# The adaLN matrices laid out transposed and summed along rows on VectorE; five weight strips opened at the start; weights stored strip by strip

## The chip, the cores and the metric

One core of a Trainium2 chip runs one launch of one kernel. The time is that of the device, in microseconds (us), from the first to the last instruction of the launch. The kernel before took 2402.32 us, the median of three runs (2398.26 to 2405.06). Layouts that numpy makes of the inputs before the launch are not in that time.

## The reference

One layer of a hybrid network, batch 1, 2048 tokens, width 1024, all float32. A vector `c` (1 x 1024) gives, through SiLU and two matrices, eight vectors of 1024: three for the mixing half, three for the feed-forward half, two for the last norm.

```
c_act = silu(c)
mod = c_act @ w_ada + b_ada                      # 1024 -> 6 x 1024
shift_m, scale_m, gate_m, shift_f, scale_f, gate_f = split(mod, 6)
h = rms_norm(x, g_norm_mix) * (1 + scale_m) + shift_m
p = h @ w_in                                     # 1024 -> 3592: 28 strips of 128 columns, and 8 columns a, beta
#   k, q, v: causal depthwise conv over 4 tokens, SiLU, gated delta rule in chunks; z gates it
#   gate_b, gate_c, h_conv: gated causal conv over 3 tokens, group norm
x = x + gate_m * (concat(ya, yb) @ w_out)
h = rms_norm(x, g_norm_ffn) * (1 + scale_f) + shift_f
gt, up = split(h @ w_gate_up, 2)                 # 1024 -> 2 x 2816
x = x + gate_f * ((silu(gt) * up) @ w_down)
shift_o, scale_o = split(c_act @ w_ada_final + b_ada_final, 2)
out = rms_norm(x, g_norm_final) * (1 + scale_o) + shift_o
```

## The kernel before

Tokens are worked in four blocks of 512. Every wide product is made of float32 operands split in two parts of the fp32r type, high and low (`whi`, `wlo` of a weight strip, `hTh`, `hTl` of the input), and three TensorE matmuls for each tile: high x high, high x low, low x high. A strip is 1024 x 128 weights; against one block of tokens it takes 8 x 3 matmuls of 128x512 into one PSUM bank (`pd`, four banks; `pm`, four more for everything else). A strip is loaded by SyncE's queue into one of four slots `wraw`, cast to `whi` by ScalarE (L389), and VectorE subtracts to get `wlo` (L391); `whi` and `wlo` have four slots each. PE's dense matmuls all stand on line L322, in a helper.

**The start.** The columns `Gm` and `Sm` (gain and shift of the first norm, feature along the partitions) need 2 x 1024 x 1024 numbers of `w_ada`. They come in three parts of 3, 3 and 2 feature blocks (`PARTS`). Of each part, eight pieces (k = 0 to 7) of 384 or 256 columns for the scale and eight for the shift are loaded. Their rows are the summed index, so VectorE multiplies each piece by a column of `silu(c)` and adds it to an accumulator (L802, L804); a matmul with ones then sums over the partitions (L483, `col_sums`). The very first part is done on TensorE instead, as 24 matmuls of one column (L796). `part_norm` then transposes the normed input (L568), ScalarE scales and shifts it in PSUM (L572) and casts it to `hTh` (L573), VectorE subtracts for `hTl` (L574). Four strips (the k heads) are "opened": after each part their matmuls for that part's feature blocks run; `proj_ab` does the 8 extra columns. After that each strip's PSUM bank goes through a convolution on VectorE (L1246, L1248 three times, L1250).

**The background.** The other six vectors are made by `mod_gen`: one piece of 128 rows x 1024 columns is loaded at each call of `fill`, between the weight strips and in the same `wraw` slots (later in the `y` slots), and added to an accumulator by VectorE (L467 first, then L469). At the end `to_col` sums over the partitions by ones (L483), or `to_row` adds the bias on one row (L505), splits the accumulator (L513) and spreads it by ones over all partitions (L516, L517, L532, L533).

**What sets the order.** Small chains of work are generators that run between the matmuls; a class `Clock` keeps a table of costs, decides by it when a generator may run, and pins the order of every engine's instructions from the k heads of the first block to the end of the mixing half. So an engine's order is fixed at build time, and an instruction that is late holds up what stands behind it. SyncE issues the loads in that order too; at most eight are under way, since each waits for the semaphore of an earlier one.

Of the kernel before, what the change touches and what calls it, by code (L numbers as in the profile page):

```python
# [40 lines left out]
HALF = 1024  # L41

# [168 lines left out]
def layer_kernel(ctx, tc, x, c, w_ada, b_ada, w_ada_final, b_ada_final, g_norm_mix, g_norm_ffn, g_norm_final,  # L211
                 w_in, conv_w_mix, conv_w_qkv, a_log, dt_bias, g_conv_out, g_dn_out, w_out, w_gate_up,
# [3 lines left out]
    w_ada, w_in, w_out, w_gate_up, w_down = w_ada[0], w_in[0], w_out[0], w_gate_up[0], w_down[0]  # L216
# [111 lines left out]
    crow = sp.tile([P, BLK], F32, name="ht", bufs=2)[:KD, :P]  # L328
    nc.scalar.dma_start(crow, c.rearrange("o (j p) -> (o j) p", p=P))
# [14 lines left out]
    nc.gpsimd.memset(g0.tile([P, 32], F32, name="pad"), 0.0)  # L344
# [3 lines left out]
    col = {}  # L348

    def columns(name, queue, rows):  # L350
        r0, n_all = 0, sum(cnt for _, _, cnt in rows)
        prow = sp.tile([P, BLK], F32, name="ht", bufs=2)[:n_all, :P]
        pc = g0.tile([P, n_all], F32, name=name)
        for n, ap, cnt in rows:
            queue.dma_start(prow[r0:r0 + cnt, :], ap)
            col[n] = pc[:, r0:r0 + cnt]
            r0 += cnt
        return prow, pc

    def turn(prow, pc):  # L360
        pt = misc_ps()
        n = pc.shape[1]
        nc.tensor.transpose(pt[:, :n], prow, ident[:n, :n])
        nc.scalar.copy(pc, pt[:, :n])

    cols_a = columns("pca", nc.scalar, [("b_ada", b_ada.rearrange("o (j p) -> (o j) p", p=P), 48),
                                        ("g_mix", g_norm_mix.rearrange("o (j p) -> (o j) p", p=P), 8),
                                        ("g_ffn", g_norm_ffn.rearrange("o (j p) -> (o j) p", p=P), 8)])
    for i, n in ((0, "b_sm"), (1, "b_cm"), (3, "b_sf"), (4, "b_cf")):
        col[n] = col["b_ada"][:, i * KD:(i + 1) * KD]  # L370

    pcs = misc_ps()
    nc.tensor.transpose(pcs[:, :KD], crow, ident[:KD, :KD])
    cs = g0.tile([P, KD], F32, name="cs")
    nc.scalar.activation(cs, epsc.to_broadcast([P, KD]), AF.Silu)
    nc.scalar.activation(cs, pcs[:, :KD], AF.Silu)
    turn(*cols_a)


    lo_engines = deque()  # L380
# [1587 lines left out]
```

## Time and profile before

| | |
|---|---|
| median of the runs shown | 2402.32 us (2398.26 to 2405.06) |
| the profiled execution's own time | 2403.85 us |
| its span in the profile | 2402.1 us |
| PE, PEld, DVE, ACT, POOL busy, share of the span | 97%, 81%, 74%, 44%, 24% |
| mean granted TensorE clock | 0.994 |
| read from and written to HBM | 265.74 MB, 75.51 MB |

PE is TensorE's matmul, PEld its weight load, DVE VectorE, ACT ScalarE, POOL GpSimd, SP SyncE. Times within the profile are us from the start of the span, where they are not marked ns. A row of a timeline gives start, duration, engine, line, operation, the tile written, the tiles read, shape and count, and in brackets the idle time before it and what ended that. A row of groups gives the count, then busy us and mean ns of one, then the idle time before. A row of windows gives the stretch and its length, then for PE, PEld, DVE, ACT and POOL the busy us and the instructions (x), then the granted clock, the busy share of the 16 DMA engines and the GB/s moved.

### The profile page before, as it was taken

Reading aid. Unit: us, or ns where it says so; the run is one execution under the profiler, and the core shown is the slowest. Engines: PE = TensorE matmul, PEld = TensorE weight load, DVE = VectorE, ACT = ScalarE, POOL = GpSimd, SP = SyncE. Lnnn points to the kernel's source line nnn. Section 1 sums busy time; section 2 is a strip of 40 time slices with the busy share of each in tenths; the row PEclk is TensorE's granted clock in tenths of the full one; section 3 lists DMA queues with packets and bytes.
Section 4 is the critical chain, followed back from the end, with each engine's and each line's share of the span. In section 5 each row is a group of like instructions: output and inputs, shape, how many; then the busy total and the mean of one; then the engine's idle time right before and its main releaser. Section 6 shows DMA issues by size and latency. Waiting matters only on the chain.

```text
span 2402.1 us, 31013 instructions
## 1 busy us (share of the span) xinstructions
PE 2341.1 (97%) x11317; PEld 1939.5 (81%) x11317; DVE 1788.3 (74%) x2673; ACT 1051.7 (44%) x1790; POOL 571.4 (24%) x643
## 2 busy tenths in 40 slices
PE   6999999999999999999999999999999999999998
PEld 5788888887888788887778888878888877887786
DVE  5988889775987678787556556875656569878888
ACT  3644664344544473366433334433333323322345
POOL 0340344033513161211000000000000036434447
PEclk9999999999999999999999999999999999999999
DMA  7443565535463445156664334753433374333433
GB/s 252 123 118 89 171 189 165 147 106 166 136 167 115 126 135 145 47 168 174 209 185 119 101 106 117 251 162 88 128 97 110 101 241 163 106 123 119 136 129 151
DMA packets 401136, 341.20 MB, mean 142 GB/s; under 512 B 39811, under 2 KB 343180, under 8 KB 400918
## 3 DMA queue, kind: packets, MB, share of 16 engines
q1 hardware_dynamic: 399430, 336.75, 45.9%
q0 software_dynamic: 1152, 2.10, 0.6%
q8 instruction: 89, 1.46, 0.2%
q14 instruction: 65, 0.53, 0.1%
q10 hardware_dynamic: 400, 0.36, 0.0%
HBM read 265.74 MB, written 75.51 MB: 142 GB/s over the span
## 4 chain that ended last, share of the span: by engine, by line
PE 66%; DVE 16%; DMA 7%; ACT 4%; issue 4%; POOL 2%; SPq 0%; ACTq 0%; DVEq 0%; POOLq 0%
PE pd L322 41%; PE pm L322 17%; DVE wlo L391 3%; DVE cv L1248 2%; DVE acc L1822 1%; DMA wraw<-in_w_in_dram 1%; ACT whi L389 1%; DMA y<-xT 1%; DVE wraw L469 1%; POOL wraw L1751 1%; DVE cv L1246 1%; PE pm L1082 1%; DMA A12d<-y 1%; DMA acc<-x 1%; PE pm L1090 1%
## 5 line engine op out<-in xcount | busy, mean ns | idle before, releaser
L389 ACT CAST whi<-wraw 128x1024 fp32r<-128x1024 f32 x286 | 299.7, 1050 | 404.5 <-PE pd L322 174.5
L391 DVE TENSOR_TENSOR wlo<-wraw,whi 128x1024 fp32r<-128x1024 f32 x286 | 361.9, 1266 | 98.4 <-ACT whi L389 94.2
L322 PE MATMUL pd<-hTh,whi 128*128 128x512 f32 x888 | 359.3, 406 | 0.6 <-ACT hTh L573 0.6
L322 PE MATMUL pd<-hTl,whi 128*128 128x512 f32 x888 | 346.9, 391 | 0.6 <-DVE hTl L574 0.6
L322 PE MATMUL pd<-hTh,wlo 128*128 128x512 f32 x888 | 347.2, 391 | 0.0
L322 PEld LDWEIGHTS pd<-hTh,wlo 128*128 128x128 f32 x888 | 166.8, 188 | 36.5 <-issue 0.3
L322 PEld LDWEIGHTS pd<-hTh,whi 128*128 128x128 f32 x888 | 167.3, 188 | 32.2 <-ACT hTh L573 1.0
L322 PEld LDWEIGHTS pd<-hTl,whi 128*128 128x128 f32 x888 | 167.6, 189 | 30.9 <-DVE hTl L574 1.1
L1616 POOL TENSOR_TENSOR wraw<-wraw 128x1024 f32<-128x1024 f32 x2 | 4.9, 2466 | 782.2 <-DMA wraw<-in_w_down_dram 773.8
L1564 DVE TENSOR_TENSOR sg<-sg,pd 128x512 f32<-128x512 f32 x44 | 30.2, 686 | 169.8 <-PE pd L322 169.8
L1822 DVE TENSOR_TENSOR acc<-acc,pd 128x512 f32<-128x512 f32 x192 | 127.4, 679 | 25.9 <-PE pd L322 24.3
L1702 ACT CAST xh<-ra 128x640 fp32r<-128x640 f32 (+1 forms) x85 | 60.4, 722 | 183.8 <-PE pm L322 134.6
L1248 DVE SCALAR_TENSOR_TENSOR cv<-pd,pcb,cv 128x511 f32<-128x511 f32 (+2 forms) x173 | 129.3, 748 | 5.2
L1711 POOL TENSOR_TENSOR xl<-ra,xh 128x640 fp32r<-128x640 f32 (+1 forms) x37 | 62.9, 1699 | 144.7 <-ACT xh L1702 144.7
L1822 DVE TENSOR_TENSOR acc<-acc,pm 128x512 f32<-128x512 f32 x120 | 81.7, 681 | 18.5 <-PE pm L322 18.1
L322 PE MATMUL pd<-whi,ym 128*128 128x512 f32 x256 | 84.8, 396 | 0.0
L1751 POOL TENSOR_TENSOR wraw<-wraw 128x512 f32<-128x512 f32 x40 | 70.0, 1772 | 46.9 <-DMA wraw<-in_w_down_dram 46.9
L322 PE MATMUL pd<-A22h,whi 128*128 128x512 f32 x176 | 70.4, 400 | 5.6 <-DVE sg L1564 5.6
L322 PE MATMUL pm<-S4h,whi 128*128 128x512 f32 x176 | 68.6, 390 | 1.3 <-ACT sg L1558 1.3
L322 PE MATMUL pd<-A22l,whi 128*128 128x512 f32 x176 | 69.7, 396 | 0.0
L322 PE MATMUL pd<-A22h,wlo 128*128 128x512 f32 x176 | 69.6, 395 | 0.0
L322 PE MATMUL pd<-S2h,whi 128*128 128x512 f32 x176 | 68.6, 390 | 1.0 <-ACT whi L389 1.0
(466 smaller groups left out, 6226.7 us busy)
## 6 DMA issues: line engine op xcount, KB each, us to landing
wraw<-in_w_in_dram SPq DMA_DIRECT2D x112, 512.0 KB
wraw<-in_w_gate_up_dram SPq DMA_DIRECT2D x88, 512.0 KB
ra<-act SPq DMA_DIRECT2D x80, 448.0 KB
wraw<-in_w_out_dram SPq DMA_DIRECT2D x40, 512.0 KB
act<-S SPq DMA_DIRECT2D x80, 256.0 KB
act<-act SPq DMA_DIRECT2D x68, 256.0 KB
wraw<-in_w_ada_dram SPq DMA_DIRECT2D x32, 512.0 KB
wraw<-in_w_down_dram SPq DMA_DIRECT2D x22, 512.0 KB
```

The source lines that it names most:

```text
L322: mm(*args, **kw)
L389: nc.scalar.copy(hi, raw)
L391: (lo_engines.popleft() if lo_engines else nc.vector).tensor_sub(lo, raw, hi.bitcast(F32))
L469: nc.vector.scalar_tensor_tensor(acc, raw, cs[:, k:k + 1], acc, op0=ALU.mult, op1=ALU.add)
L1082: mm(py[:, j * P:(j + 1) * P], Mm[h][:, j, :], T[h][:, j, :], start=True, stop=True)
L1090: mm(pz[:, j * P:(j + 1) * P], Y[h][:, j, :], Xs[h][:, j, :], start=True, stop=True)
L1248: nc.vector.scalar_tensor_tensor(cv[:, n - t:], u[:, :BLK - n + t], taps[t], cv[:, n - t:], op0=ALU.mult, op1=ALU.add)
L1564: nc.vector.tensor_add(s5[i], s5[i], a[i])
L1702: nc.scalar.copy(hi, raw[:, c0:c1, :])
L1711: eng.tensor_sub(lo, raw, hi.bitcast(F32))
L1751: nc.gpsimd.tensor_mul(r[:, hs], r[:, hs], gate_f[:, hs])
L1822: nc.vector.tensor_add(accs[s, u][:, ns], accs[s, u][:, ns], ps)
```

## The change

**Layout by numpy.** `laid_out` stacks `w_ada` and `w_ada_final` into one array of eight matrices, transposed: `w_ada[v, k]` holds feature block k of vector v with the output feature along the partitions and the 1024 summed inputs along the row. All bias, gain and convolution columns come as one array `cols` of 128 x 145. The weights `w_in`, `w_out`, `w_gate_up` are stored strip by strip, so that a partition's part of a strip is 4 KB in one piece, where it was eight pieces of 512 B (two of 2 KB for `w_out`).

**Sums along rows.** `sums_of` is one VectorE instruction: the 128x1024 block times a row of `silu(c)` that stands in all partitions, with the sum of each partition's row as a second output, a column. Nothing is summed over partitions any more: `col_sums`, the ones matmuls, `cs`, `turn` are gone. Two small ScalarE instructions for each block then make its column of `Gm` and `Sm`. A row that is needed in all partitions (`gate_m`, `gate_f`, and two for the last norm) is written as a column to DRAM and loaded back as a row. The row of `silu(c)` is kept in DRAM (`c_d`) and loaded again at the start of every `mod_gen`; it takes the slot that the accumulator had.

**The start.** The loop runs feature block by feature block (8 steps, not 3 parts): load of a pair of blocks (1 MB), two sums, scale, split, and at once the matmuls of that block for all strips opened so far. Five strips are opened, the fifth in the tile `yal` with a `pm` bank, and the last block of each is done in the main loop (`LAST`).

```diff
+    def sums_of(raw, row, total):
+        nc.vector.scalar_tensor_tensor(raw, raw, 1.0, row, op0=ALU.mult, op1=ALU.mult, accum_out=total)
-    def mod_gen(w, c0, fin):
-        acc = temp()
+    def mod_gen(v, fin):
+        row = temp()
+        clock.kept.add(row.name)
+        nc.sync.dma_start(row, c_d.to_broadcast([P, D]))
+        sums = g0.tile([P, KD], F32, name="ms", bufs=2)
         for k in range(KD):
             raw = temp()
-            nc.sync.dma_start(raw, w[k * P:(k + 1) * P, c0:c0 + D])
-            if k == 0:
-                nc.vector.tensor_scalar_mul(acc, raw, cs[:, 0:1])
-            else:
-                nc.vector.scalar_tensor_tensor(acc, raw, cs[:, k:k + 1], acc, op0=ALU.mult, op1=ALU.add)
+            nc.sync.dma_start(raw, w_ada[v, k])
+            sums_of(raw, row, sums[:, k:k + 1])
             yield
...
+    def to_row(sums, bias, t):
+        nc.vector.tensor_add(sums, sums, bias)
+        nc.sync.dma_start(t.rearrange("o (k p) -> p (o k)", p=P), sums)
...
     def col_strip(w, c0):
         shape = [P, KD, P]
-        return split_w(raw_w(w[:, c0:c0 + P].rearrange("(k p) n -> p k n", p=P), shape), shape)
+        return split_w(raw_w(w[c0 // P], shape), shape)
...
+        def ada_load(k):
+            t = ap_.tile([P, 2, D], F32, name=PLACES[k % 4])
+            nc.sync.dma_start(t, w_ada[0:2, k].rearrange("s p n -> p s n"))
+            return t
+
+        def ada_sums(k, raw):
+            sums_of(raw[:, 1], crow, totals[1][:, k:k + 1])
+            sums_of(raw[:, 0], crow, totals[0][:, k:k + 1])
+            nc.scalar.activation(Gm[:, k:k + 1], totals[1][:, k:k + 1], AF.Identity,
+                                 scale=col["g_mix"][:, k:k + 1], bias=gb[:, k:k + 1])
+            nc.scalar.activation(Sm[:, k:k + 1], totals[0][:, k:k + 1], AF.Identity, bias=col["b_sm"][:, k:k + 1])
...
+        nc.scalar.dma_start(crow, c.to_broadcast([P, D]))
+        nc.scalar.activation(crow, crow, AF.Silu)
+        nc.scalar.dma_start(c_d, crow[0:1, :])
...
+        for k in range(KD):
+            ada_sums(k, raws[k])
+            ps = turned
+            if k + 1 < KD:
+                turned = transpose_k(xt0, k + 1)
+            scale_split(ps, k, Gm, Sm, *hT)
+            if k + 4 < KD:
+                raws.append(ada_load(k + 4))
+            if k == 0:
+                strips.append(next(reqs)[0](w_in, 2048 + 3 * P))
+            if k == 1:
+                strips.append(fifth())
+            if k <= NH:
+                pre.append((strips[k], dense_ps() if k < NH else misc_ps()))
+            if k + 1 < KD:
+                for h in range(len(pre)):
+                    proj(pre[h][1], pre[h][0], *hT, ks=range(0 if h == k else k, k + 1))
...
-                        proj(ps, w, hh, hl, PARTS[2])
+                        proj(ps, w, hh, hl, LAST)
...
-                        fill(h + 1)
+                        fill(min(NH - len(pre), PRE + 1))
```

How the orders move, at the two places that matter below. **VectorE from the first pieces of `w_ada` on**; `ym`, `kd`, `vt`, `yah`, `yal`, `zs` are tiles that hold loaded pieces for the while, `gate_m` and `zs` are accumulators. Before, the first twelve rows of that stage:

```order
L813 TENSOR_TENSOR Gm<-pm,pca 128x3
L814 SCALAR_TENSOR_TENSOR Gm<-Gm,pca 128x3
L802 TENSOR_SCALAR gate_m<-kd,cs 128x384
L804 SCALAR_TENSOR_TENSOR gate_m<-kd,cs,gate_m 128x384 x3
L804 SCALAR_TENSOR_TENSOR gate_m<-vt,cs,gate_m 128x384 x4
L823 TENSOR_TENSOR Sm<-pm,pca 128x3
L391 TENSOR_TENSOR wlo<-wraw,whi 128x1024 x2
L574 TENSOR_TENSOR hTl<-pm,hTh 128x512
L391 TENSOR_TENSOR wlo<-wraw,whi 128x1024
L574 TENSOR_TENSOR hTl<-pm,hTh 128x512
L391 TENSOR_TENSOR wlo<-wraw,whi 128x1024
L574 TENSOR_TENSOR hTl<-pm,hTh 128x512
```

Now, from the first sums on (here `gate_m` holds the row of `silu(c)`, `ms` the sums; L438 is `sums_of`, L369 the strip's low part, L499 the input's):

```order
L438 SCALAR_TENSOR_TENSOR kd,ms<-kd,gate_m 128x1024 x2
L369 TENSOR_TENSOR wlo<-wraw,whi 128x1024
L438 SCALAR_TENSOR_TENSOR vt,ms<-vt,gate_m 128x1024 x2
L499 TENSOR_TENSOR hTl<-pm,hTh 128x512
L369 TENSOR_TENSOR wlo<-wraw,whi 128x1024
L499 TENSOR_TENSOR hTl<-pm,hTh 128x512
L438 SCALAR_TENSOR_TENSOR yah,ms<-yah,gate_m 128x1024 x2
L369 TENSOR_TENSOR wlo<-wraw,whi 128x1024
L499 TENSOR_TENSOR hTl<-pm,hTh 128x512
L438 SCALAR_TENSOR_TENSOR zs,ms<-zs,gate_m 128x1024 x2
L438 SCALAR_TENSOR_TENSOR kd,ms<-kd,gate_m 128x1024
L499 TENSOR_TENSOR hTl<-pm,hTh 128x512
```

The pieces are wider, every feature block has its two sums, and the low part of a block's input stands right behind the next block's sums.

**TensorE at the end of the start**, where the last feature blocks come in. Before (L483 the ones matmuls, L568 the transposes, L833 and L834 the 8 extra columns):

```order
L834 MATMUL pm<-hTl,wabs 16x512
L483 MATMUL pm<-ones_r,zs 128x16 x2
L483 MATMUL pm<-ones_r,gate_m 128x16 x2
L568 MATMUL pm<-ck,kq 128x128 x8
L363 MATMUL pm<-ck,ht 128x65
L833 MATMUL pm<-hTh,wabs 16x512
L322 MATMUL pd<-hTh,whi 128x512
```

Now (L493 the transposes, L324 dense, L717 and L718 the extra columns), around the transposes of the last block:

```order
L717 MATMUL pm<-hTh,wabs 16x512
L718 MATMUL pm<-hTl,wabs 16x512
L493 MATMUL pm<-ck,kq 128x128 x4
L324 MATMUL pd<-hTh,whi 128x512
L324 MATMUL pd<-hTl,whi 128x512
L324 MATMUL pd<-hTh,wlo 128x512
L324 MATMUL pd<-hTh,whi 128x512
L324 MATMUL pd<-hTl,whi 128x512
L324 MATMUL pd<-hTh,wlo 128x512
L324 MATMUL pd<-hTh,whi 128x512
L324 MATMUL pd<-hTl,whi 128x512
L324 MATMUL pd<-hTh,wlo 128x512
```

The transposes of the last block stand ahead of the matmuls of the block before it, three for each of the four strips in `pd` banks and then, below these rows, three for the fifth strip and two for the extra columns; no ones matmul stands between the last sums and the last block's matmuls.

More of the change, by code (lines that the diff above doesn't have):

```diff
@@ L343, in layer_kernel @@
     nc.vector.memset(epsc, EPS)
-    nc.gpsimd.memset(g0.tile([P, 32], F32, name="pad"), 0.0)
     nc.gpsimd.memset(gr.tile([P, 504], F32, name="pad"), 0.0)
[L348 to L377, printed above, removed]
+    pc = g0.tile([P, NCOLS], F32, name="pc")
+    nc.scalar.dma_start(pc, cols)
+    col, at = {}, 0
+    for n, cnt in COLS:
+        col[n] = pc[:, at:at + cnt]
+        at += cnt
+    gb = g0.tile([P, KD], F32, name="gb")
+    nc.vector.scalar_tensor_tensor(gb, col["b_cm"], 1.0, col["g_mix"], op0=ALU.add, op1=ALU.mult)
     lo_engines = deque()
```

225 lines of the change are left out of this document (73 added, 152 removed).

## Prediction

> **What bounds the kernel now.** I read the page's busy shares first, then windows by stage, then the timeline of the start, since most of the change stands there.
>
> ```profile
> PE 2341.1 (97%) x11317; PEld 1939.5 (81%) x11317; DVE 1788.3 (74%) x2673; ACT 1051.7 (44%) x1790; POOL 571.4 (24%) x643
> 0.00:28.20 28.20, 15.08 (x68) 14.37 (x68) 7.32 (x17) 13.76 (x21) 4.05 (x16) 1.00 0.95 313
> 28.20:66.20 38.00, 30.86 (x137) 23.34 (x137) 25.37 (x51) 12.70 (x23) 0.57 (x2) 0.87 0.53 167
> 66.20:82.00 15.80, 13.34 (x56) 10.64 (x57) 14.78 (x33) 8.60 (x13) 7.72 (x11) 0.89 0.29 77
> 82.00:150.00 68.00, 67.78 (x337) 56.48 (x336) 66.83 (x109) 40.88 (x80) 31.48 (x31) 1.00 0.48 130
> 150.00:200.00 50.00, 48.16 (x233) 39.98 (x232) 40.88 (x94) 20.60 (x44) 10.22 (x15) 1.00 0.58 142
> ```
>
> TensorE is busy 97% of the span, so after the start a gain must take work off PE or make its queue begin sooner. The first 82 us are another matter. Up to 28.2 PE's busy time is hardly dense work; from 28 to 82 it works at a granted clock of 0.87 to 0.89. VectorE is full from 66 to 150 us (14.78 of 15.80, 66.83 of 68.00), PE from 82 on: both bound that stretch, and from 150 on VectorE has 9 us to spare in 50 while PE has 2. The timeline shows what the start waits for:
>
> ```profile
> 7.75 10.40 PE L796 MATMUL pm<-cs,ym 128*128 128x1 f32 x48 [0.23 <-ACT cs L376]
> 28.26 0.73 PE L322 MATMUL pd<-hTh,whi 128*128 128x512 f32 x2 [0.58 <-ACT hTh L573]
> 59.29 0.16 DVE L813 TENSOR_TENSOR Gm<-pm,pca 128x2 f32<-128x2 f32 x1 [5.25 <-PE pm L483]
> 62.19 1.29 DVE L574 TENSOR_TENSOR hTl<-pm,hTh 128x512 fp32r<-128x512 f32 x2 [2.23 <-ACT hTh L573]
> 66.28 0.75 DVE L1246 TENSOR_SCALAR cv<-pd,pcb 128x512 f32<-128x512 f32 x1 [0.62 <-PE pd L322]
> ```
>
> The first dense matmul is at 28.26; the input's last low part (`hTl`) ends at 63.5; the first convolution starts at 66.28. VectorE waited 5.25 us for the ones matmuls, which stood in PE's queue behind the open strips. So the start is a chain of loads, sums and splits, and 66.28 is the moment to compare.
>
> **The change, part by part.** *The chain of the start.* Prices:
>
> ```profile
> 0.00:10.00 10.00, 2.83 (x13) 2.61 (x13) 0.58 (x4) 4.07 (x9) 2.11 (x12) 1.00 0.78 250
> 10.00:20.00 10.00, 8.14 (x39) 8.06 (x38) 1.64 (x5) 5.92 (x8) 1.94 (x5) 1.00 0.98 332
> L469 DVE SCALAR_TENSOR_TENSOR wraw<-wraw,cs x28: 1273/1280/2395, 78.1 to 637.4; 128x1024 f32<-128x1024 f32 x28
> L574 DVE TENSOR_TENSOR hTl<-pm,hTh 128x512 fp32r<-128x512 f32 x8 | 5.3, 687 | 2.7 <-ACT hTh L573 2.7
> L391 DVE TENSOR_TENSOR wlo<-wraw,whi 128x1024 fp32r<-128x1024 f32 x4 | 4.9, 1224 | 1.6 <-DMA yal<-in_w_ada_dram 1.4 <-ACT whi L389 0.3
> L572 ACT ACTIVATE pm<-pm,Sm,Gm 128x512 f32<-128x512 f32 x8 | 6.0, 757 | 24.3 <-PE pm L568 24.2
> L573 ACT CAST hTh<-pm 128x512 fp32r<-128x512 f32 x8 | 4.5, 592 | 0.1
> L773 ACT ACTIVATE kq<-kq,ss 128x1024 f32<-128x1024 f32 x4 | 4.5, 1143 | 3.0 <-POOL ss L540 3.0
> L545 ACT ACTIVATE ht<-kq 128x1024 bf16<-128x1024 f32 x4 | 4.2, 1053 | 3.8 <-DMA kq<-in_x_dram 2.0 <-PE pm L373 1.8
> 1275.40 5.44 PE pd L322 x24
> ```
>
> Ahead of and with the first pair of blocks stand x (2.10 MB), the row of c in all partitions (0.52), two small tables (0.14) and the pair (1.05): 3.81 MB. The start moved 2.50 MB in its first 10 us, then 332 GB/s: 3.81 MB at 13.9 us, and VectorE's sums begin at about 14. Its list from there is 16 sums, 5 `wlo`, 8 `hTl`: 16 x 1.28 + 5 x 1.22 + 8 x 0.69 = 32.1 us, to 46.1 with no wait. The waits, by the new order: the first `wlo` stands behind a `whi` cast that ScalarE reaches only after four squares, one SiLU of the same width and most of the scalings (about 1.5 us late); each `hTl` needs two small ScalarE operations (0.2 each, an estimate from the 0.16 us VectorE row above), L572 and L573 after its own block's sums, 1.8 us, of which the work placed between covers all but 0.3 to 0.8 in blocks 0 to 5 (3 us in all); the last block has one `hTl` for cover (1.1). So the last `hTl` ends near 52, where it was 63.5.
>
> PE then still has block 6's matmuls of five strips (15), four of the extra columns and three of block 7 before the first convolution can start: 22 x 0.227 (24 in 5.44 us) = 5.0 us, from about 50.6, when block 6's `hTl` is there. The first convolution starts at **55.5, 10.8 us sooner**. The other loads do not hold this up: 13.8 MB at 332 GB/s would be there by 44 us, the last pair needed at 48.5.
>
> *VectorE after that, to 150.* With VectorE full there, its list sets the time. Taken out: one `wlo` (the fifth strip's is made early), 1.2 us, and `to_row` of `gate_m`:
>
> ```profile
> L505 DVE TENSOR_TENSOR wraw<-wraw 1x1024 f32<-1x1024 f32 x1 | 1.2, 1206 | 0.0
> L513 DVE TENSOR_TENSOR wraw<-wraw 128x512 fp32r<-128x512 f32 x2 | 1.4, 684 | 0.0
> ```
>
> That is 2.6 us, 3.8 together. The seven sums left of `gate_m` replace seven L469 at the same base price. What the second output costs no VectorE row shows. Bounds: nothing (the inputs and the write are L469's, so nothing is gained), and 1.28 us more (the sum done as two passes). The nearest row is ScalarE's own accumulating square, whose read-out is a separate record:
>
> ```profile
> L545 ACT ACTIVATION_READ_ACCUMULATOR ht<-kq 128x1 f32 x4 | 0.7, 187 | 0.0
> ```
>
> I take half of it, 0.1 us, because ScalarE's overlap their main instruction: 23 sums x 0.1 = 2.3 us lost. The start is worth 10.8 + 3.8 - 2.3 = **12.3 us**. After the five strips PE waits for the sixth: its `whi` slot comes free with the first strip's last matmul, and its `wlo` now stands behind a convolution and the head chain. That is some 6 us, from 58 to 64 (an estimate: a convolution is four operations like L1246 at 0.75, the head chain some twenty like L813 at 0.16, then 1.2), paid by PE's lead over VectorE (below); without the lead it would be 6 us of loss.
>
> *PE's list later.* The ones matmuls are taken away from a full engine:
>
> ```profile
> L483 PE MATMUL pm<-ones_r,wraw 128*128 128x16 f32 x32 | 3.7, 257 | 0.0
> L516 PE MATMUL pm<-wraw,ones_r x4: 394/394/494, 132.6 to 674.9; 128*128 128x512 f32 x4
> L533 PE MATMUL pm<-ht,ones_r x4: 392/396/399, 1720.9 to 1931.8; 128*128 128x512 f32 x4
> ```
>
> 3.7 us for `Gf` and `Sf`. A row costs four matmuls of 0.227; `gate_m`'s lie in the stretch that VectorE sets, the other three rows give 12 x 0.227 = 2.7. Together **6.4 us**. The casts and subtractions that go with them were beside PE and count nothing; with ScalarE at 44% that cover holds. The new writes of a column to DRAM and back stand in SyncE's queue with two weight loads between them, and the rows are used over 50 us later; if a load were held by one, it would be a few us once.
>
> *Weights in 4 KB pieces.*
>
> ```profile
> 20.00:25.00 5.00, 1.42 (x7) 1.43 (x8) 3.35 (x6) 1.58 (x2) 0.00 (x0) 1.00 1.13 347
> 1970.00:1975.00 5.00, 4.11 (x18) 3.42 (x19) 4.86 (x7) 1.14 (x2) 2.29 (x3) 1.00 1.03 418
> 1100.00:1250.00 150.00, 144.81 (x639) 117.83 (x640) 93.82 (x127) 78.33 (x110) 4.66 (x8) 0.99 0.69 209
> 1540.00:1600.00 60.00, 57.49 (x245) 46.73 (x244) 45.43 (x55) 20.63 (x28) 0.00 (x0) 0.97 0.57 177
> ```
>
> At 20 to 25 us strips in 512 B pieces come at 347 GB/s, at 1970 us rows of 4 KB at 418. Only where PE idles can that count: 5.2 us in 1100 to 1250 and 2.5 in 1540 to 1600. Bounds: nothing, and those 7.7. I take 1, since most of those loads are not weights. The Trainium skill ("DMA: Bandwidth & Descriptors", Specifications) puts the smallest transfer for line rate at 512 B; by it the layout would bring nothing and the sum would be 1 us less, while the two rows differ by a fifth.
>
> **The sum.** 12.3 + 6.4 + 1 = 19.7 off the profiled execution's 2403.85: 2384.1. That execution stands 1.5 us above the median of the runs, so I predict **2383 us**.
>
> **Rivals.** *PE's lead carries over.* Windows of L322 alone count the dense matmuls:
>
> ```profile
> 0.00:66.20 66.20, 19.78 (x78) 15.12 (x78) 0.92 0.71 229
> 0.00:81.10 81.10, 31.55 (x120) 24.15 (x121) 0.92 0.63 200
> ```
>
> Five strips (120 matmuls) were done at 81.1, now at 55.5 + 12 x 0.227 = 58.2: 23 us sooner, against VectorE's 14.6 (10.8 + 3.8). If VectorE's background work can slip past 150, where it has 9 us to spare, the start gives up to 23: 2403.85 - 23 - 7.4 - 1.5 = 2372. Against it: both engines are full to 150, the order is fixed, and only four `pd` banks stand between them. 16%.
>
> *The loads hold the start.* If the pairs come at the first 10 us' 250 GB/s throughout, 13.8 MB are there at 55 us, the last `hTl` ends near 60: 3 us gained, not 10.8. The start is then worth 3 + 3.8 - 0.7 = 6, the total 13.4: 2389. For it: the pairs are the widest loads yet, and a place is loaded again only after its sums. Against it: 332 GB/s in the second window, 418 for rows of 4 KB. 14%.
>
> *Slower: the sum with a second output takes two passes' time*, 2.56 us. VectorE then has 23 x 1.28 = 29.4 us more in the stretch that it sets; the start turns from 14.6 gained to 14.8 lost, and with 7.4 gained later the time is 2403.85 - 1.5 + 7.4 = 2410. The point from which this decides is a sum of (14.6 + 7.4) / 23 = 0.96 over the base, 2.24 us. For it: both inputs are float32 in SBUF, as in L469, which already takes 1.28 us where a one-input operation of the same width (L467) takes less:
>
> ```profile
> L467 DVE TENSOR_SCALAR wraw<-wraw,cs x4: 748/748/753, 53.3 to 568.8; 128x1024 f32<-128x1024 f32 x4
> ```
>
> Against it: L469 has the same two inputs and writes as much. 9%. The Trainium skill ("Vector Engine (DVE) Microarchitecture Reference", Points that are easy to get wrong) says that this form with two SBUF sources that are not bf16 runs at half throughput, with no port left to read the accumulator back. By that rule the 2410 of this rival holds, unless L469's price has the halving in it already; no row of the profile has this form with an accumulator.
>
> *The start's gain is given back.* The first block's inverse goes through DRAM:
>
> ```profile
> 151.67 3.64 DMA dm<-Dg
> 155.95 6.56 DMA yal<-dm
> ```
>
> If PE reaches its end sooner but the chain behind these two does not, the lead is waited out, and only what leaves PE's list stays: 2403.85 - 1.5 - 7.4 = 2395, no change that can be told. Against it: the chain begins at the extra columns, which also come some 9 us sooner. 9%.
>
> **How the numbers follow.** My forecast, VectorE's list setting the start, 52%; its own range is 2375 to 2391 (last `hTl` between 49 and 57, read-out between 0 and 0.19). With the rivals at 2372, 2389, 2410 and 2395 the range for 8 in 10 is **2367 to 2400**: it leaves out the slower case and little on the other side. A measurement of this kernel can tell about 0.3%, 7 us, from no change. Faster than 2395: 52 + 16 + 12 of the loads' 14 = 80%; within: the given-back case and 2 of the loads, 11%; slower: 9%.
>
> **What would show it.** In the profile of the changed kernel: the sums at 1.28 to 1.5 us each; VectorE from 14 us on nearly without gaps; the last `hTl` near 52 and the first convolution near 55.5; PE waiting between 58 and 64 and again for VectorE up to 130; the end of the VectorE-full stretch 12 to 15 us sooner than before; no ones matmul after it, and PE's busy time there 6 us less. The prediction is wrong if the first convolution starts after 62, if a sum takes over 2.2 us, or if PE's idle time after 150 grows by more than 10 us.

## The result and the profile after

The changed kernel took **2441.38 us** (median, 2436.84 to 2442.45), the kernel before 2402.87 beside it: ratio **1.0159, 95% interval 1.014 to 1.0179**. It is slower by 38.5 us where 19.7 less were forecast. The page of the changed kernel (profiled execution 2436.84 us, span 2435.0) has for the engines:

```profile
PE 2333.2 (96%) x11192; PEld 1925.8 (79%) x11192; DVE 1782.0 (73%) x2697; ACT 1041.9 (43%) x1784; POOL 568.5 (23%) x642
```

TensorE has 7.9 us less to do than before (2341.1), as planned. But its idle time is 101.8 us (span less busy time) where it was 61.0. The two profiled spans differ by 32.9 us, so all of the loss is new waiting. The start is not where it waits. The timeline of VectorE (start, duration, line, tile, idle time before):

```profile
12.92 1.23 DVE L438 SCALAR_TENSOR_TENSOR kd<-kd,gate_m 128x1024 f32<-128x1024 f32 x1 [6.10 <-DMA kd<-in_w_ada_dram]
14.07 0.08 DVE L438 DVE_READ_ACCUMULATOR kd<-kd,gate_m 128x1 f32 x1
14.07 1.22 DVE L438 SCALAR_TENSOR_TENSOR kd<-kd,gate_m 128x1024 f32<-128x1024 f32 x1
52.84 0.69 DVE L499 TENSOR_TENSOR hTl<-pm,hTh 128x512 fp32r<-128x512 f32 x1 [3.51 <-ACT hTh L498]
56.42 0.75 DVE L1159 TENSOR_SCALAR cv<-pd,pc 128x512 f32<-128x512 f32 x1
```

Sums begin at 12.92, the last `hTl` ends at 53.5, the first convolution starts at 56.42, 9.9 us sooner than the 66.28 before. The loss lies later. Windows, first of the kernel before, then of the changed one (stretch, length, then PE, PEld, DVE, ACT, POOL, the granted clock, DMA share, GB/s):

```profile
230.00:250.00 20.00, 20.00 (x137) 18.19 (x135) 15.11 (x23) 5.52 (x19) 6.62 (x16) 1.00 0.17 54
250.00:270.00 20.00, 19.60 (x118) 16.85 (x118) 15.49 (x17) 13.48 (x27) 8.21 (x16) 1.00 0.46 158
540.00:580.00 40.00, 39.99 (x189) 31.03 (x188) 21.21 (x25) 15.92 (x22) 9.29 (x7) 1.00 0.52 153
1580.00:1610.00 30.00, 28.20 (x117) 22.82 (x116) 22.62 (x26) 9.85 (x13) 0.00 (x0) 0.94 0.54 161
```

```profile
230.00:250.00 20.00, 16.86 (x145) 14.49 (x144) 14.69 (x18) 7.89 (x19) 2.53 (x6) 1.00 0.28 79
250.00:270.00 20.00, 15.18 (x93) 12.92 (x92) 9.37 (x14) 5.04 (x18) 5.25 (x9) 0.91 0.09 23
540.00:580.00 40.00, 32.65 (x159) 26.63 (x159) 17.05 (x21) 19.37 (x34) 9.48 (x14) 0.89 0.25 77
1600.00:1630.00 30.00, 19.84 (x76) 15.88 (x76) 17.89 (x28) 6.60 (x9) 0.14 (x1) 0.77 0.67 181
```

TensorE now idles at the ends of the first two blocks, where little but the serial chain of the delta rule is left (it inverts a triangular matrix: small diagonal blocks are taken through DRAM and back, the round trip below, and the "level" matmuls then join them), and again in the feed-forward half near 1600 us, and the granted clock falls to 0.77 to 0.91 in three of these four rows. Three places, and as the runs show, three different causes.

### The profile page after: what moved, and what is told of

The parts are those of the page before. It is cut to its first block, busy times and chain, and to the rows that moved or that the text cites. A ratio compares the mean times of both kernels' runs of the same rounds, so it can differ in the third digit from the quotient of the medians.

```text
span 2435.0 us, 30701 instructions
## 1 busy us (share of the span) xinstructions
PE 2333.2 (96%) x11192; PEld 1925.8 (79%) x11192; DVE 1782.0 (73%) x2697; ACT 1041.9 (43%) x1784; POOL 568.5 (23%) x642
## 4 chain that ended last, share of the span: by engine, by line
PE 65%; DVE 16%; DMA 8%; ACT 5%; issue 4%; POOL 3%; SPq 0%; DVEq 0%; POOLq 0%; ACTq 0%
PE pd L324 41%; PE pm L324 17%; DVE wlo L369 3%; DVE cv L1161 2%; DMA y<-in_w_ada_dram 1%; DVE acc L1733 1%; DMA y<-xT 1%; DVE wraw L438 1%; ACT whi L367 1%; DMA wraw<-in_w_in_dram 1%; DVE cv L1159 1%; DVE cv L1234 1%; DMA A12d<-y 1%; PE pm L1003 1%; PE pm L995 1%
## 5 line engine op out<-in xcount | busy, mean ns | idle before, releaser
L369 DVE TENSOR_TENSOR wlo<-wraw,whi 128x1024 fp32r<-128x1024 f32 x285 | 361.0, 1268 | 102.7 <-ACT whi L367 100.4
L324 PE MATMUL pd<-hTh,whi 128*128 128x512 f32 x888 | 360.6, 407 | 1.4 <-ACT hTh L498 1.3
L324 PE MATMUL pd<-hTh,wlo 128*128 128x512 f32 x888 | 349.5, 394 | 5.9 <-DVE wlo L369 5.9
L324 PE MATMUL pd<-hTl,whi 128*128 128x512 f32 x888 | 348.6, 393 | 0.0
L324 PEld LDWEIGHTS pd<-hTh,wlo 128*128 128x128 f32 x888 | 168.0, 189 | 44.0 <-DVE wlo L369 7.9
L324 PEld LDWEIGHTS pd<-hTh,whi 128*128 128x128 f32 x888 | 168.6, 190 | 34.2 <-ACT hTh L498 1.9
L324 PEld LDWEIGHTS pd<-hTl,whi 128*128 128x128 f32 x888 | 168.6, 190 | 31.0 <-DVE hTl L499 0.4
L1613 ACT CAST xh<-ra 128x640 fp32r<-128x640 f32 (+1 forms) x85 | 60.4, 722 | 184.4 <-PE pm L324 138.9
L1161 DVE SCALAR_TENSOR_TENSOR cv<-pd,pc,cv 128x511 f32<-128x511 f32 (+2 forms) x173 | 129.3, 748 | 5.2
L324 PE MATMUL pd<-whi,ym 128*128 128x512 f32 x256 | 89.2, 409 | 9.7 <-ACT ym L1150 9.7
L324 PE MATMUL pd<-A22h,whi 128*128 128x512 f32 x176 | 70.2, 399 | 13.8 <-DVE sg L1475 13.8
L324 PE MATMUL pm<-S1h,whi 128*128 128x512 f32 x176 | 69.4, 394 | 1.2 <-ACT whi L367 1.2
L324 PE MATMUL pd<-S2h,whi 128*128 128x512 f32 x176 | 69.3, 394 | 1.0 <-ACT whi L367 1.0
L324 PE MATMUL pd<-S2h,wlo 128*128 128x512 f32 x176 | 69.3, 394 | 0.5 <-DVE wlo L369 0.5
```

Source lines behind the costliest of these rows:

```text
L324: mm(*args, **kw)
L369: (lo_engines.popleft() if lo_engines else nc.vector).tensor_sub(lo, raw, hi.bitcast(F32))
L1161: nc.vector.scalar_tensor_tensor(cv[:, n - t:], u[:, :BLK - n + t], taps[t], cv[:, n - t:], op0=ALU.mult, op1=ALU.add)
L1613: nc.scalar.copy(hi, raw[:, c0:c1, :])
```

## The experiments

Times are medians; each ratio is to the kernel before measured beside it, with its 95% interval. Prices in us are differences of ratios times 2400; such a difference is uncertain by 0.002 to 0.003, 5 to 7 us. Where an expectation's range and a time are compared, the kernel before stood between 2398 and 2403 us in all runs.

| run | what | us | ratio |
|---|---|---|---|
| e1_rows32 | change, row writes of 32 bytes | 2426.55 | 1.0107 (1.0089 to 1.0124) |
| e2_before_writes | before, four column writes added | 2406.60 | 1.0023 (1.0014 to 1.0033) |
| e4_back | old start, new background | 2427.67 | 1.0115 (1.0098 to 1.0133) |
| e3b_start | new start, old background | 2443.95 | 1.0175 (1.0160 to 1.0191) |
| e8_pad | the same, weights' tiles back in place | 2405.54 | 1.0035 (1.0022 to 1.0048) |
| e11_start4 | the same with four strips | 2392.29 | 0.9963 (0.9949 to 0.9977) |
| e5_pause | change, two pauses | 2432.10 | 1.0127 (1.0109 to 1.0144) |
| e6_four | change, four strips | 2425.45 | 1.0105 (1.0082 to 1.0129) |
| e10_mix | e1, another claim on chain buffers | 2420.13 | 1.0090 (1.0072 to 1.0107) |
| e7_three | change, 32 bytes, pauses, four strips | 2395.03 | 0.9965 (0.9953 to 0.9976) |
| e12_writes | change, pauses and four strips | 2409.95 | 1.0037 (1.0024 to 1.0049) |
| e9_layout | before, weights by strips | 2396.36 | 0.9991 (0.9980 to 1.0002) |

### The writes of single numbers

In the changed kernel `gate_m`'s column of 128 x 8 goes to DRAM at 110.94 us as 1,024 pieces of 4 bytes. Behind it in SyncE's queue stand two weight strips. The chain of work around it (start, duration, what), the wait of SyncE's queue (us in all, times, longest), and windows of 2 us:

```profile
110.94 0.38 SPq L460
111.38 13.93 DMA wraw<-in_w_in_dram
SPq L785 <- DMA gate_md<-ms: 10.3, 1, 10.3
112.00:114.00 2.00, 2.00 (x17) 1.83 (x16) 1.97 (x5) 1.95 (x6) 1.28 (x1) 1.00 0.96 31
114.00:116.00 2.00, 2.00 (x11) 1.67 (x10) 1.97 (x3) 1.99 (x4) 0.00 (x0) 1.00 0.20 6
116.00:118.00 2.00, 2.00 (x10) 1.65 (x10) 1.93 (x5) 0.94 (x6) 0.00 (x0) 1.00 0.65 45
120.00:122.00 2.00, 1.93 (x15) 1.60 (x14) 1.97 (x5) 0.00 (x0) 1.92 (x2) 1.00 0.48 25
124.00:126.00 2.00, 1.40 (x7) 0.81 (x5) 0.00 (x0) 0.67 (x1) 1.12 (x5) 1.00 1.04 322
```

For 10 us the DMA engines move 6 to 45 GB/s (the stretch from 112 to 122) and are still shown busy for a good part of it. A strip issued right behind the write takes 13.93 us, where the page's median is 4.2. Its cast on ScalarE and all that is queued behind that come late, and VectorE stands still from 124 to 126. The Trainium skill ("DMA: Bandwidth & Descriptors", Queues, rings and completion order) says that each DMA engine takes the descriptors of a ring (the entries of its list, one for each piece) in order, and that a transfer's semaphore rises only after every earlier write of that engine. The trace agrees: SyncE's wait of 10.3 us for the write ends at 122.9 us and the strip behind it lands at 125.3, both at the end of the hole. Whether the strips behind the write cost the time here, or SyncE's own wait before it can issue the loading back (L785), no run separates; at 1594 us, below, there is no such wait, and the load behind the write is late all the same.

**e1_rows32** takes the small pieces away and nothing else:

```diff
-        nc.sync.dma_start(t.rearrange("o (k p) -> p (o k)", p=P), sums)
+        nc.sync.dma_start(t.rearrange("o (p k) -> p (o k)", p=P), sums)
...
-    given["w_ada"] = ada.T.reshape(8, KD, P, D)
+    given["w_ada"] = ada.T.reshape(8, KD, P, D).copy()
+    for v in (2, 5, 6, 7):
+        given["w_ada"][v] = ada.T[v * D:(v + 1) * D].reshape(P, KD, D).transpose(1, 0, 2)
...
+    for n in ("b_gm", "b_gf", "b_so", "b_go"):
+        parts[n] = parts[n].reshape(P, KD).T
```

> The changed kernel with one thing altered: for the four vectors that become rows, the host lays the matrix out so that partition p of sum k holds feature 8p+k, and the write of the sums to DRAM is 128 pieces of 32 bytes in the place of 1,024 pieces of 4 bytes. All instructions, their order and all other transfers stay. Theory 1 (the writes of 4-byte pieces hold up the transfers behind them, 10 us or so at each of the four places, and what waits for those): the hole of traffic at 113 to 122 us goes, the two strips issued at 111 us land within 5 us in the place of 13.9, and the time falls from 2441 to 2385 to 2415. Theory 2 (the order fixed for the first two blocks, with the start's lead in it, lets TensorE use up its dense work too soon; the writes are a side matter): 2430 to 2441.

Measured: 1.0107, by the ratios 12.5 us less than the change (1.0159 - 1.0107, times 2400). The same windows in this run:

```profile
112.00:114.00 2.00, 2.00 (x17) 1.79 (x16) 1.97 (x5) 1.95 (x6) 1.28 (x1) 1.00 0.68 145
114.00:116.00 2.00, 2.00 (x12) 1.67 (x11) 1.97 (x3) 1.99 (x4) 0.00 (x0) 1.00 1.06 389
116.00:118.00 2.00, 2.00 (x11) 1.65 (x10) 1.93 (x4) 0.98 (x6) 0.00 (x0) 1.00 0.96 336
gate_md<-ms SPq DMA_DIRECT2D x1, 4.0 KB, 2.0
```

The hole is gone and the write lands in 2.0 us. The first theory holds for these writes, but the time lies between the two ranges: most of the loss is elsewhere. Whether the number of pieces or their size counts is not separated, since both changed eightfold.

**e2_before_writes** puts four such writes, to DRAM vectors that nothing reads, into the kernel before:

```diff
     def to_row(acc, bias_row, put):
+        nc.sync.dma_start(waste.pop().rearrange("o (k p) -> p (o k)", p=P), Gm)
```

> The kernel before, and nothing changed but that at each of its four row conversions one more transfer is issued on SyncE's queue: 1,024 pieces of 4 bytes from an SBUF tile of 128 x 8 to a DRAM vector that nothing reads. Theory 1: each holds up the weights behind it by about 10 us, of which the two free strips cover a part: 2403 becomes 2420 to 2445. Theory 2: nothing waits for these writes, 2403 to 2408.

Measured: 1.0023, 5.5 us, in the range of the second theory. But the writes did not go where the expectation put them. SyncE's rows of this run:

```profile
60.37 0.38 SPq L505 DMA_DIRECT2D waste<-Gm  x1
61.42 1.41 SPq L505 DMA_DIRECT2D waste<-Gm  x2
569.03 0.43 SPq L505 DMA_DIRECT2D waste<-Gm  x1
```

Three of the four are issued from 60.4 to 62.8 us, as soon as `Gm` is there, and not at a row's conversion; from 60 to 70 us the kernel before moves 1 GB/s, so there is next to nothing that they could hold up. Only the fourth stands among the loads. So the 5.5 us are no price of a write in its real place, and the run decides between neither theory. **e12_writes** gives the price in a kernel whose other causes are taken away; it differs from e7_three below in the pieces of 4 bytes alone:

> The changed kernel with four strips and the two pauses, and the row writes in pieces of 4 bytes as the change has them; beside the run with all three alterations (0.9965 of the kernel before) it prices the four writes in a kernel that is otherwise mended. They cost 12 us in the change and 6 in the kernel before. If the price is that of the traffic behind them and each is paid: 2403 to 2411, 1.001 to 1.004. If it was a matter of the other two causes: 2390 to 2398.

Measured: 1.0037 against 0.9965, **17 us** for four writes, in the range of being paid each. In the feed-forward half the write for the last norm also holds the next piece of `w_ada`: its load took 12.96 us in the changed kernel, and VectorE's sums there (second and third row, from the groups of the changed kernel and of e1_rows32) waited 17.2 and 9.5 us in all:

```profile
1594.27 12.96 DMA y<-in_w_ada_dram
L438 DVE SCALAR_TENSOR_TENSOR y<-y 128x1024 f32<-128x1024 f32 x16 | 19.5, 1222 | 17.2 <-DMA y<-in_w_ada_dram 17.2
L438 DVE SCALAR_TENSOR_TENSOR y<-y 128x1024 f32<-128x1024 f32 x16 | 19.4, 1221 | 9.5 <-DMA y<-in_w_ada_dram 9.5
```

### Start and background apart

**e4_back** is the kernel before with the new `mod_gen`, `to_col` and `to_row` (the transposed matrix is given beside the old one):

```diff
-        bg.append(mod_gen(w_ada, 2 * D, lambda acc: to_row(acc, b_ada[:, 2 * D:3 * D], row_tile(gate_m))))
+        bg.append(mod_gen(2, gate_row))          # and the five others alike
```

> The old start and the old layout of the weights with the new background work: six vectors summed along rows of the transposed matrix, and the four writes of 1,024 pieces of 4 bytes. Theory 1: 2420 to 2450. Theory 2 (the loss needs the start's lead): 2395 to 2408, since the background's VectorE list is a little shorter.

Measured: 1.0115. The background alone costs 27.6 us, with the old start, so the second theory's range (2395 to 2408) is out.

**e3b_start** is the reverse, the new start with the old background. (A first form of it, e3_start, needed 64 bytes a partition more than SBUF had left and gave no time.)

```diff
-        bg.append(mod_gen(2, gate_row))          # and the five others alike
+        bg.append(mod_gen(w_adaN, 2 * D, lambda acc: to_row(acc, b_ada[:, 2 * D:3 * D], row_tile(gate_m))))
```

> The new start with five strips and the new layout of the weights, with the old background work (accumulators, rows by TensorE, pauses, no column written to DRAM); the host also gives c as a column, for the old sums. Theory A (the lead of the start is given back in the first block, nothing is lost behind it): 2397 to 2408. Theory B (the start keeps its 10 us, all loss is the background's): 2383 to 2393.

Measured: 2443.95, a miss for both theories. The dense matmuls at 1700 to 1900 us took 395 ns each, where the kernel before and the change have 389. Tiles stand one behind the other in SBUF, and the edit had shortened what lies ahead of the weights by 32 bytes (the first `whi` stands at byte 26,592 of a partition, where it was 26,624). **e8_pad** puts them back:

```diff
+    g0.tile([P, 8], F32, name="pad")
     pc = g0.tile([P, NCOLS], F32, name="pc")
```

> The kernel of the new start with the old background (2443.95), with one unused tile of 32 bytes a partition put ahead of the column tile; instructions, order and transfers stay. In that kernel every dense matmul took 395 ns in the place of 389 and the weights' tiles stood 32 bytes lower than in the kernel before and in the change, at addresses that are not a multiple of 64. If the place of the weights is the cause: 389 ns again, 6 ns of each of 9,024 matmuls or some 40 to 54 us less, 2390 to 2404. If the dense matmuls were slower for another reason (the order, the transfers): 2440 to 2447.

Measured: 2405.54, and the groups of the two runs (e3b_start first) show the matmul's price:

```profile
L324 PE MATMUL pd<-A22h,wlo 128*128 128x512 f32 x40 | 15.8, 395 | 0.0
L324 PE MATMUL pd<-A22h,wlo 128*128 128x512 f32 x44 | 17.1, 389 | 0.0
```

The 389 ns came back as expected; the time is just past the range, since the gain was 34 to 38 us and not the 40 to 54 expected. So the new start with five strips, the weights by strips in it, costs **+8.4 us** by itself (1.0035), not the 12.3 gained that the prediction had. With the background's 27.6 that makes 36.0 of the 38.5. **e11_start4** opens four strips:

> The new start with the old background and the weights' tiles where they were (2405.5, 1.0035 of the kernel before), with four strips opened in the place of five. Theory A (the fifth strip is what turns the start's gain into a loss, 12 to 16 us as in the change): 2388 to 2394, 0.994 to 0.998 of the kernel before. Theory B (the fifth strip only hurts together with the new background): 2402 to 2408.

Measured: 0.9963, in the range of theory A. The start as such gains **8.9 us**, and the fifth strip turns that into a loss of 8.4: it costs 17 us.

### The fifth strip

**e6_four** does the same to the changed kernel:

```diff
-            if k == 1:
-                strips.append(fifth())
-            if k <= NH:
+            if k < NH:
```

> The changed kernel with four strips opened in the place of five; all else as in the change, with the 4-byte writes. Theory A (the fifth strip gives TensorE dense work that it needs later, beside the first block's serial chain, and its part of VectorE's list stands ahead of that chain): the DRAM round trip of the diagonal blocks starts 6 to 10 us sooner than the 149 of the change, and 2441 becomes 2426 to 2433. Theory B (a strip opened sooner can only help, the first block loses for another reason): 2441 to 2450.

Measured: 1.0105, 13 us less, a little better than the range of theory A. Timelines and windows of this run, then the chain's first step on VectorE and the round trip in the changed kernel:

```profile
51.52 0.75 DVE L1157 TENSOR_SCALAR cv<-pd,pc 128x512 f32<-128x512 f32 x1
104.64 0.68 DVE L915 TENSOR_TENSOR kd<-pm,eg 128x512 f32<-128x512 f32 x1
133.69 0.38 SPq L938 DMA_DIRECT2D dm<-Dg  x1
230.00:250.00 20.00, 20.00 (x128) 17.94 (x127) 17.66 (x22) 12.39 (x25) 10.29 (x18) 1.00 0.50 164
250.00:270.00 20.00, 18.36 (x96) 14.73 (x94) 14.55 (x18) 19.75 (x33) 4.14 (x7) 1.00 0.48 153
```

```profile
119.17 0.69 DVE L917 TENSOR_TENSOR kd<-pm,eg 128x512 f32<-128x512 f32 x1
149.16 0.38 SPq L940 DMA_DIRECT2D dm<-Dg  x1
0.00:149.16 149.16, 121.98 (x559) 96.52 (x560) 116.23 (x203) 77.05 (x159) 42.58 (x61) 0.97 0.58 190
```

```profile
0.00:133.69 133.69, 110.01 (x509) 87.75 (x510) 109.39 (x198) 80.47 (x153) 41.17 (x60) 0.97 0.62 207
```

With four strips the first convolution starts 4.9 us sooner still (51.52), and the round trip of the diagonal blocks through DRAM starts at 133.7, not 149.2 (15 us sooner, where 6 to 10 were expected); TensorE idles for 1.6 of the 40 us from 230, where the changed kernel leaves 8.0. The fifth strip is ready work for TensorE, but the serial chain does not need it so early. In the order made with it, from the first convolution on, VectorE has eleven convolutions and ten low parts ahead of the chain's first step there (`kd<-pm,eg`, at 119.17 us); with four strips it has nine and nine, and the step comes at 104.64. By the round trip both kernels have done all twelve convolutions, so only 6.8 of the 15.5 us are more work of VectorE (busy for 116.23 us with five strips and 109.39 with four, windows of the changed kernel, then of this run); the rest is waiting. The lead that the fifth strip gives TensorE is dense work that is missing at 240 to 270 us, beside the bare chain. The same shows without the small writes, in e8_pad and then e11_start4:

```profile
230.00:250.00 20.00, 14.18 (x123) 12.03 (x121) 13.41 (x19) 6.45 (x22) 4.37 (x10) 0.99 0.15 50
230.00:250.00 20.00, 20.00 (x123) 17.44 (x122) 18.62 (x24) 10.46 (x24) 11.09 (x21) 1.00 0.47 158
```

From 200 to 300 us TensorE is busy for 90.0 us in e8_pad and 97.7 in e11_start4. That is 7.7 us of the 9.2 by which the two profiled executions differ; of the 17 us between the medians it is about half, and the rest is not placed.

Another reading was possible. In e1_rows32 the inverse's transposes end at 201.6, but TensorE's level matmuls begin at 212.1, behind dense work, since a mixing chain held two of the six buffers of chain work when the order was made. **e10_mix** changes that claim:

```diff
                 yield from wait("mx", 1)
+                if b == 0 and m >= 1:
+                    yield from wait("inv", 2)
                 yield from take("cv", 1)
```

> The changed kernel with row writes in pieces of 32 bytes (first run, 2426.6), and one rule of the host's plan added: in the first block, mixing chains 1 to 3 claim their two of the six buffers of chain work only once the inverse is done. In the first run the inverse's transposes end at 201.6 but TensorE's level matmuls stand behind 10 us of dense work, since the third mixing chain holds the last two buffers. Theory C (that claim is what the first block's chain loses): 2410 to 2418. Theory A (the fifth strip's share of VectorE and the dense work it spends early are the loss, so TensorE only runs out of dense work elsewhere): 2422 to 2428.

Measured: 1.0090, 4 us less than e1_rows32 by the ratios, which is within their uncertainty. The time itself lies between the two ranges; the ratio times 2400.5, the kernel before beside e1_rows32, gives 2422.1, the lower end of theory A. The rows of the level matmuls (e1_rows32, then this run) and this run's windows:

```profile
212.09 3.73 PE L995 MATMUL pm<-lv,ym 128*128 128x128 f32 x32
198.71 3.73 PE L995 MATMUL pm<-lv,ym 128*128 128x128 f32 x32
230.00:250.00 20.00, 16.80 (x100) 14.23 (x98) 18.51 (x24) 8.12 (x17) 6.68 (x12) 1.00 0.35 106
250.00:270.00 20.00, 15.87 (x98) 14.48 (x99) 12.21 (x17) 5.71 (x14) 5.57 (x9) 0.83 0.48 158
```

The level matmuls come 13.4 us sooner, and TensorE still idles 7.3 of the 40 us after 230 (8.1 in e1_rows32). The claim does hold the level matmuls up, but it is not what the block loses.

### The pauses

The old `to_col` and `to_row` paused (`settled`) until their matmuls could run, and in that time `fill` started no new sums. The change dropped the matmuls and with them the pauses. **e5_pause** gives them back, without work in them:

```diff
+        for _ in range(2):
+            yield
         clock.kept.discard(row.name)
         fin(sums)
```

> The changed kernel with one thing given back that it removed without saying so: each of the six background vectors pauses for two strips between its last sum and its end (the kernel before waited there for its matmuls). All sums, writes and loads stay as in the change. Theory A (in the second block the two vectors now follow each other without a pause, nine sums in the place of six stand on VectorE inside the inverse chain, and the fixed order is made for that): the second block's loss goes, 2441 becomes 2425 to 2431. Theory B (the sums themselves and their writes cost, wherever they stand): 2438 to 2443.

Measured: 1.0127, 7.7 us less than the change, in the direction of the first theory, just past its range, and not far clear of the uncertainty. VectorE's groups and its windows from the second block's beginning to the end of its inverse: before, change, this run.

```profile
L469 DVE SCALAR_TENSOR_TENSOR wraw<-wraw,cs 128x1024 f32<-128x1024 f32 x10 | 15.8, 1576 | 2.4 <-DMA wraw<-in_w_ada_dram 2.4
L467 DVE TENSOR_SCALAR wraw<-wraw,cs 128x1024 f32<-128x1024 f32 x2 | 1.5, 748 | 0.0
302.00:429.00 127.00, 127.00 (x644) 104.92 (x643) 112.56 (x223) 69.78 (x140) 56.38 (x64) 1.00 0.59 175
```

```profile
L438 DVE SCALAR_TENSOR_TENSOR wraw<-wraw 128x1024 f32<-128x1024 f32 x16 | 24.8, 1548 | 1.1 <-DMA wraw<-in_w_ada_dram 1.1
309.00:448.40 139.40, 135.90 (x669) 111.52 (x668) 124.31 (x251) 71.37 (x141) 58.85 (x64) 1.00 0.61 190
```

```profile
L438 DVE SCALAR_TENSOR_TENSOR wraw<-wraw 128x1024 f32<-128x1024 f32 x14 | 19.0, 1360 | 1.2 <-DMA wraw<-in_w_ada_dram 1.2
309.00:441.90 132.90, 131.02 (x652) 107.59 (x651) 116.19 (x240) 69.32 (x140) 56.38 (x64) 1.00 0.58 181
540.00:580.00 40.00, 40.00 (x193) 32.60 (x192) 22.52 (x25) 16.97 (x24) 7.67 (x6) 1.00 0.42 138
```

In the change all 16 sums of the two vectors stand on VectorE before the second block's inverse is done, 24.8 us, where 12 (two of them the short form) took 17.3; with a convolution more as well it has 12 us more to do there, and the stretch is 12 us longer. With the pauses two sums move behind it, the stretch shrinks by 6.5 us, and TensorE is full at 540 to 580, where the change leaves 7.3 us empty. About half of the 5.8 us that the sums take less is in the two sums; the other 14 also ran shorter, 1.36 us against 1.55, and why is not shown. The expectation counted nine sums in the change and six before, inside the inverse alone; over the stretch that sets the time it is 16 and 12, and 14 with the pauses.

### The three together, and the layout

**e7_three** has the pieces of 32 bytes, the pauses and four strips at once:

> The changed kernel with three alterations at once: the row writes in pieces of 32 bytes (first run), the two pauses, and four strips. Theory A (three causes that add, 15 us for the writes as the first run showed, and 12 to 13 for each of the others): 2390 to 2403, level with the kernel before or a little under it. If they do not add (the second and third are one loss, seen twice): 2405 to 2418.

Measured: 0.9965, 2395.0 us, **faster than both kernels**. One at a time the three gave 12.5, 7.7 and 13 us; together they give 46.6. The 13 us over their sum (33.2) are as large as its uncertainty, since all three are taken from the same measurement of the change; whether they help each other is not shown. Left open too are 5.3 us of idle TensorE from 1050 to 1100 (1.6 before), where SyncE waits for a transfer of the block before (19.4 us for `x<-cv`); e11_start4, with the old background, has the same wait (19.5).

e7_three and e11_start4 differ, but for a few small tiles, in the background alone: new with its causes mended, and old. Their pages:

```profile
PE 2324.1 (97%) x11192; PEld 1920.9 (80%) x11192; DVE 1776.7 (74%) x2697; ACT 1049.3 (44%) x1790; POOL 569.1 (24%) x642
PE 2332.4 (97%) x11240; PEld 1926.5 (80%) x11240; DVE 1785.2 (74%) x2657; ACT 1058.3 (44%) x1805; POOL 568.2 (24%) x642
```

The new background leaves TensorE 8.3 us less to do, and the ratios are 0.9965 and 0.9963: it gains nothing, with some 4 us of uncertainty. The whole gain over the kernel before is that of the start and of the weights by strips.

**e9_layout** is the kernel before with the weights by strips:

```diff
-        return split_w(raw_w(w[:, c0:c0 + P].rearrange("(k p) n -> p k n", p=P), shape), shape)
+        return split_w(raw_w(w[c0 // P], shape), shape)          # w_out and w_gate_up alike
```

> The kernel before with the weights of w_in, w_out and w_gate_up laid out by strips and nothing else. The prediction counted 1 us for it. Theory: the strips were not late before (their transfers took 4 us with 2 strips of lead), 2398 to 2404. Rival (pieces of 4 KB in the place of 512 bytes free the DMA engines where transfers bind): 2385 to 2397.

Measured: 0.9991 (0.9980 to 1.0002): 2 us or nothing. The time of 2396.36 would fall in the rival's range, but the kernel before beside it took 2398.14.

## Why the prediction was wrong

Of the sum's 19.7 us, 12.3 were to come from the start and 6.4 from the background. By themselves the start lost 8.4 us and the background 27.6. Point by point, by the prediction's own steps:

- **The chain of the start: right at its ends, in part by luck.** Last `hTl` near 52 (53.5), first convolution 55.5 (56.42), 10.8 us sooner (9.9). Three errors offset each other between: the sums began at 12.92 us, not 14; VectorE was busy for 29.8 us up to the last `hTl`, not 32.1; and its waits for ScalarE's casts were 10.9 us (7.8 before `hTl`, 3.1 before `wlo`), where 5.6 were counted. So "nearly without gaps" did not hold.
- **The sums' price: right, on the cheap side.** 1.22 us and a read-out of 0.08 that overlaps; from one sum's start to the next 1.15 us, not 1.38. The slower rival, a sum of 2.56 us, did not occur. The rule of the Trainium skill that stood with it ("Vector Engine (DVE) Microarchitecture Reference", Points that are easy to get wrong) has this form, with two SBUF sources that are not bf16, at half throughput; here nothing beyond L469's own price was halved, since the form with an accumulator takes less than the 1.28 us of L469 without one.
- **PE's list: right as work, wrong as time.** 6.4 us less forecast, 7.9 us less on the page. The sum took these 6.4 us off the time because the engine is full. No run shows that gain: with its causes mended the new background is level with the old one (e7_three against e11_start4), though TensorE has 8.3 us less to do. What takes them back stays open.
- **Weights in 4 KB pieces: not contradicted.** 1 us taken, 2 us or nothing measured.
- **"if a load were held by one, it would be a few us once": the step that failed first.** I looked at when the rows are used, 50 us later, and not at what stands behind the write in the same rings. It held the loads behind it for some 10 us at both places looked at (112 and 1594 us); the four writes cost 12.5 us in this kernel, 17 in the mended one. The price of such a write was nowhere in the trace of before; I should have bounded it from above by its 1,024 pieces (the profile counts 1,093 packets under 512 B from 108 to 126 us, 254 with pieces of 32 bytes) and by the two strips behind it.
- **The fifth strip: mis-sized, with the wrong sign.** The sum credited it with a `wlo` less (1.2 us) and let "PE's lead over VectorE" pay for the wait that followed. That wait came, but TensorE idles as long without the fifth strip (5.0 us from 55 to 70 us in e8_pad, 4.8 in e11_start4). The price was elsewhere, in the chain that the order put back and in the cover it lost: 17 us (e8_pad against e11_start4). The rival "PE's lead carries over" asked whether the lead lasts; the question was what it is made of.
- **"the first block's inverse chain" rival** ("the start's gain is given back", 2395, 9%) named the right place. In e8_pad the round trip starts 7.2 us sooner than before (144.43 against 151.67), and the lead is still waited out, from 230 us on; with the fifth strip it went past zero to +8.4, with four it did not happen.
- **"The end of the VectorE-full stretch 12 to 15 us sooner": wrong**, by the writes and the fifth strip. VectorE has gaps in it now, and the round trip of the diagonal blocks starts at 149.16, 2.5 us sooner than before (151.67). Without the small pieces it is 144.35 (e1_rows32), with four strips 133.69.

```profile
82.00:150.00 68.00, 64.77 (x333) 53.79 (x332) 60.05 (x101) 35.71 (x91) 30.47 (x32) 0.97 0.51 139
```

- **What was not in the sum at all**: the pauses that left with `settled`. The change was costed by its instructions; a generator's pause is no instruction, yet it spaced VectorE's work in a stretch that VectorE sets. It is worth 7.7 us in this kernel.
- Of "what would make the prediction wrong", the last came true: TensorE's idle time after 150 us grew by 36.5 us (38.1 to 74.6).

## What to carry to other kernels

A small transfer is to be priced by its pieces and by what is queued behind it, not by its bytes and its reader: four writes of 1,024 pieces of 4 bytes cost here more than the start, with four strips, had gained. Work taken off a full engine is not yet time: here 8 us of it brought nothing. Work brought forward helps only where it shortens the chain that ends last; where it is cover taken from beside that chain, it is lost. Where an order is fixed by a planner, a pause in a generator belongs on the list of what a change removes. And where the order is not pinned, an added instruction goes where its inputs allow: look in the trace for where an experiment's edit really stands.

## What the runs showed of the hardware that was not expected

- Behind a write of 1,024 pieces of 4 bytes the core's traffic fell to 6 to 45 GB/s for 10 us. As 128 pieces of 32 bytes the same 4 KB landed in 2.0 us with no hole.
- With the weights' tiles 32 bytes lower in SBUF, no longer at a multiple of 64, the dense matmuls from 1700 to 1900 us took 395 ns, not 389. Over 9,024 matmuls the two runs differ by 38 us (2443.95 and 2405.54, ratios 1.0175 and 1.0035 give 34). The two kernels differ in nothing else than 32 bytes of unused tile; it moves every tile behind it, the weights' among them, while `hTh` and `hTl`, which lie elsewhere, stay. That 64 bytes is the grain was not tested.
